# Seven products instead of eight for 81 pairs of row blocks, and a build-time planner for side work

## The chip, the cores and the metric

The kernel runs on one core of a Trainium2 chip. The metric is the device time of one execution in microseconds (us); three runs of the kernel before gave 1948.49 to 1948.88 us, median 1948.88. The engines are TensorE (PE, with its weight loads as PEld), VectorE (DVE), ScalarE (ACT), GpSimd (POOL) and SyncE (SP), which issues most loads.

## The reference

One encoder layer over 256 tokens with 4096 features, all in float32:

```python
h = rms_norm(x, g_mix)
c_q, c_kv, k_rope, gate_a, q_b, k_b, v_b, gate_b = split(h @ w_in)     # 4096 x 11840
q_a = rms_norm(c_q, g_q_latent) @ w_uq                                 # 16 heads, 128 + 64 rotary
k_nope, v_a = split(rms_norm(c_kv, g_kv_latent) @ w_ukv)
y_a = rms_norm(mla_attention(q_a, k, v_a), g_out_mla) * silu(gate_a)
y_b = rms_norm(dilated_mixture(q_b, k_b, v_b), g_out_dil) * silu(gate_b)
x = x + concat(y_a, y_b) @ w_out                                       # 4096 x 4096
gate = sigmoid(rms_norm(x, g_ple) @ w_ple_gate)                        # 4096 x 4096
out = rms_norm(x + (p @ w_ple) * gate, g_final)
```

## The kernel before

Every product of two float32 matrices is made from three matmuls in a faster 32-bit format. Both operands are split into a rounded part hi and a rest lo, and `mm` (L133 to L135) adds hi x hi, hi x lo and lo x hi in PSUM. Splitting is the side work that never ends: ScalarE copies the weights to hi (L115), VectorE subtracts to get lo (L116). A weight tile holds 1024 columns on 128 partitions.

Weights stream through a list of steps. Each step has a load into one of four raw buffers, a split into a slot of a ring (three slots, in places some spare buffers more), and a run on TensorE. The main loop at the end runs the steps in order and splits the weights of a later step after each (two steps ahead, up to five where the ring is longer). All engines take their instructions in the order in which the build emits them.

Steps of the older kind (`Chunk`) multiply both row tiles of the 256 tokens with up to 512 columns. The wide products are `Block`s of 1024 columns. In a block a *plain* step takes one row block of 128 weight rows in four products (12 matmuls of 512 columns). A *fast* pair takes two row blocks in seven products instead of eight, by the Strassen-Winograd scheme, as four steps with 3, 6, 6 and 6 matmuls, 21 for what two plain steps do in 24. For that, VectorE forms four differences of weight quarters (`sub`, L780), splits of these replace part of the plain splits, and the other operand needs sums made beforehand (`add_sums`, L818). The eight results of a block go to eight PSUM banks; a middle step (`d_mid` for the q, k and v blocks, opened by the copy in L636) empties four of them after the last fast step, and an end step (`d_done`, L651) the rest.

The order of stages: the latent columns (four chunks), the first gate chunk, the uq stage (the up projections of queries and keys, with the second gate chunk strewn in and the attention heads beside it; `done_uq` ends a query chunk with a copy in L478 and a rotary part that ends in L493; the heads' exponentials are in L417), two more gate chunks, six D blocks (q, k, v, in two halves), four gate chunks of the second kind with the dilated attention beside, three output blocks and two chunks, three gate blocks of the last product, and a tail.

Side work (attention heads, normalisations, turning tiles) is written as generators. `advance`, called after every step, resumes each of them once: what they emit, and when, is decided by the number of steps alone. Transposes go alternately to two PSUM banks (`turn_bank`). Fast pairs stand where a string says so, as four steps in a row, for example

```python
order = mix("CCCCSCSCSCSCSCSC" if n < 5 else "CCCCCSCCSCCSCCSC")     # S: a fast pair, C: two plain steps
```

Of the kernel before, what the change touches and what calls it, by code (L numbers as in the profile page):

```python
# [65 lines left out]

class Chunk:
# [4 lines left out]
    def __init__(self, src, nk, n, lhs, banks, done, needs=lambda j: (), per=2, ts=(0, 1), keep=None):  # L72
        self.src, self.nk, self.n, self.lhs, self.banks = src, nk, n, lhs, banks
        self.done, self.needs, self.per, self.ts, self.keep = done, needs, per, ts, keep
        self.ps = None
# [3 lines left out]
def encoder_layer(ctx: ExitStack, tc: tile.TileContext, x, p, positions, g_mix, w_in, g_q_latent, w_uq,  # L79
                  g_kv_latent, w_ukv, g_out_mla, g_out_dil, w_out, w_ple, g_ple, w_ple_gate, g_final,  # L80
                  c_inv, c_dist, out):
    nc = tc.nc
# [11 lines left out]
    def slot(tag, shape, dtype=F32):  # L94
        names[tag] = names.get(tag, 0) + 1
        return sp.tile([P, *shape], dtype, tag=tag, name=f"{tag}_{names[tag]}")

    def bank(tag, shape, bufs=1):
        names[tag] = names.get(tag, 0) + 1
        return pp.tile([P, *shape], F32, tag=tag, name=f"{tag}_{names[tag]}", bufs=bufs)  # L100
# [40 lines left out]
    make_identity(nc, ident)  # L141
# [25 lines left out]
    def turn_gains(i, at, n):  # L167
        tp = turn_bank([2 * S])
        nc.tensor.transpose(tp[:, :n], gains[:n, i], ident[:n, :n])
        yield  # L170
        nc.scalar.activation(gT[:, at:at + n], tp[:, :n], AF.Copy)

# [61 lines left out]
    flags, urgent, waiting, running = set(), [], [], []  # L234
    ticks = [0, -9]

    def spawn(task):
# [71 lines left out]
    def turn_c(bs):  # L309

        for b in bs:
            tp = turn_bank([2, S])
# [6 lines left out]
            split_rows(*(q[:, o:o + 2] for q in cT[key]), tp, G[key][:, o:o + 2])  # L319
            yield  # L320

    def done_a(i):
        def task(ps):
# [7 lines left out]
            for t in range(NT):  # L331
# [3 lines left out]
                else:  # L335
                    nc.scalar.activation(dst, ps[t], AF.Copy, scale=rx[:, t:t + 1])
            yield
# [26 lines left out]
    def latents():  # L364
# [8 lines left out]
        for _ in range(3):  # L373
            yield
        tp = turn_bank([2, S])
# [3 lines left out]
        split(pe[:, 0], pe[:, 1], tp[:, 0])  # L379
        flags.add("kpe")  # L380
# [5 lines left out]
    def attend(h, q_src, k_src, pe, v, y, dil):  # L386
# [4 lines left out]
        tp = turn_bank([4, P])  # L391
        for t in range(NT):
            nc.tensor.transpose(tp[:, t], q_src(t), ident)
            nc.tensor.transpose(tp[:, NT + t], k_src(t), ident)
        yield
        qk = slot(f"T{h % 2}", [2, 4 * P], F32R)
        split(qk[:, 0], qk[:, 1], tp.rearrange("p a b -> p (a b)"))
        if dil:
            flags.add(("read", h))
        yield  # L400
        s = bank("s", [NT, S])
        for t in range(NT):
# [3 lines left out]
            if pe is not None:  # L406
                both = pe[0]()[:, t * P:(t + 1) * P]
                nc.tensor.matmul(s[:, t], both, pe[1][0], start=False, stop=False)
                nc.tensor.matmul(s[:, t], both, pe[1][1], start=False, stop=True)
        yield  # L410
        i = h % 2
        e = E["t"][:, i]
        nmax, l, rl = E["s"][:, i, 0], E["s"][:, i, 1], E["s"][:, i, 2]
        if not dil:
            nc.vector.tensor_reduce(nmax, s, axis=AX.X, op=ALU.max, negate=True)
            for t in range(NT):
                nc.scalar.activation(e[:, t], s[:, t], AF.Exp, bias=nmax[:, t:t + 1], accum_out=l[:, t:t + 1])  # L417
        else:
            flat = "p a b -> p (a b)"
            nc.vector.scalar_tensor_tensor(e.rearrange(flat), E["d"][:, 0].rearrange(flat), -SLOPES[h],  # L420
                                           s.rearrange(flat), op0=ALU.mult, op1=ALU.add)
            nc.vector.tensor_reduce(nmax, e, axis=AX.X, op=ALU.max, negate=True)
# [17 lines left out]
        tp = turn_bank([NT, S])  # L440
        for k in range(NT):
            for t in range(NT):
                nc.tensor.transpose(tp[:, k, t * P:(t + 1) * P], e[:, t, k * P:(k + 1) * P], ident)
        yield
        pt = slot(f"T{2 + h % 2}", [2, NT, S], F32R)
        split(pt[:, 0], pt[:, 1], tp)
        if dil:
# [4 lines left out]
        o = bank("o", [S])  # L452
        for k in range(NT):
            mm(o, v(k), tuple(pt[:, i, k] for i in range(2)), k == 0, k == NT - 1)
        yield
# [3 lines left out]
        if h:  # L459
            nc.gpsimd.tensor_tensor(acc, acc, sq, op=ALU.add)  # L460
        flags.add(("head", dil, h))
# [10 lines left out]
    def done_uq(i):  # L472
        def task(ps):
# [3 lines left out]
            for t in range(NT):  # L477
                nc.scalar.activation(q[:, t].rearrange("p h c -> p (h c)"), ps[t], AF.Copy, scale=rqs[:, t:t + 1])  # L478
            both = kq[:, 512:].rearrange("p (t h d r) -> p t h d r", t=NT, h=2, d=2)
            rotate(both[:, :, :, 0], q[:, :, :, NOPE:], both[:, :, :, 1], 2)  # L480
            yield
            yield
            nc.scalar.activation(both[:, :, :, 1], both[:, :, :, 0], AF.Copy)
            yield
            tp = turn_bank([2, S])
# [4 lines left out]
            yield  # L490
            pe = slot("Q0", [2, S], F32R)
            nc.scalar.activation(pe, tp, AF.Copy)
            nc.vector.tensor_tensor(pe[ROPE:], tp[ROPE:], plain(pe[ROPE:]), op=ALU.subtract)  # L493
            pairs[i]["pe"] = pe
# [3 lines left out]
    def done_uk(i):  # L498
        def task(ps):
# [8 lines left out]
            for t in range(NT):  # L508
# [3 lines left out]
                split(v[:, 0, t], v[:, 1, t], kv[:, :, 1], sc)  # L512
            for hh in range(2):
                h = 2 * i + hh
                waiting.append(({("uq", i)}, attend(
# [5 lines left out]
                    y_rows(ya, h), False), 2))  # L521
# [10 lines left out]
    def y_stats(dil):  # L532
        while not all(("head", dil, h) in flags for h in range(HEADS)):
            yield
        yield
        tp = turn_bank([2 * S])
# [3 lines left out]
        yield from rsqrt_mean(ry[dil], tp[:, :NT], WIDTH)  # L540
        nc.vector.tensor_tensor(ry[dil], ry[dil], rxh, op=ALU.mult)
        flags.add(("ry", dil))

    U_TAGS = ("B7a", "B7b", "T5", "T6"), ("T7", "B7a", "B7b", "T4")

    def done_gate(dil, c):
        def task(ps):
            u = slot(U_TAGS[dil][c], [NT, 512])
            for t in range(NT):
                nc.scalar.activation(u[:, t], ps[t], AF.Tanh, scale=rxh[:, t:t + 1])  # L550
                nc.vector.scalar_tensor_tensor(u[:, t], u[:, t], 1.0, ps[t], op0=ALU.add, op1=ALU.mult)
                yield
            while ("ry", dil) not in flags or (c and ("turned", dil, c - 1) not in flags):
                yield
            yield
            for t in range(NT):
                nc.scalar.activation(u[:, t], u[:, t], AF.Copy, scale=ry[dil][:, t:t + 1])
            yield
            for b in range(2):
                w = u[:, :, S * b:S * (b + 1)]  # L560
                tp = turn_bank([2, S])
                for k in range(2):
                    for t in range(NT):
                        nc.tensor.transpose(tp[:, k, t * P:(t + 1) * P], w[:, t, k * P:(k + 1) * P], ident)
                if b:
                    flags.add(("turned", dil, c))
                yield
                for k in range(2):
                    h = 4 * c + 2 * b + k
                    g = G["ob" if dil else "oa"][:, h:h + 1]  # L570
                    y = yb_rows(h) if dil else by_token(y_rows(ya, h))
                    nc.vector.scalar_tensor_tensor(by_token(w[:, k]) if dil else y, y, g, by_token(tp[:, k]),
                                                   op0=ALU.mult, op1=ALU.mult)
            if not dil:
                flags.add(("gated", c))
                return
            while (("yT", 0, 3) if c == 0 else ("yT", 1, 1)) not in flags and c != 1:
                yield
            if c == 2:
                yt = [slot(b, [4, S], F32R) for b in ("B7a", "T6")]  # L580
            else:
                both = slot({0: "B3", 1: "B5", 3: "B6"}[c], [2, 4, S], F32R)
                yt = [both[:, 0], both[:, 1]]
            yT[4 + c] = yt
            for b in range(2):
                yield
# [829 lines left out]
```

## Time and profile before

| | |
|---|---|
| median of three runs | 1948.88 us |
| the profiled execution, first to last instruction | 1948.2 us |
| PE, PEld | 1926.8 us (99%), 1638.7 us (84%) |
| DVE, ACT, POOL | 1448.6 us (74%), 1062.6 us (55%), 67.9 us (3%) |
| DMA | 370.57 MB, 190 GB/s |
| chain that ended last | PE 90%, DVE 5%, ACT 3%, issue 1%, DMA 1% |

Matmuls are pipelined, so a matmul's recorded duration is longer than the distance to the next one's start, and a busy PE may still be waiting. Rows of the time line have the start and the duration in us, the engine, the source line, the operation, what it writes and reads with buffer numbers left out, the form, and in brackets the engine's idle time before it and what ended it. Rows of grouped instructions have a count, the total busy time in us, the mean duration in ns and the idle time before them. Waits have the total in us, how often, and the longest.

### The profile page before, as it was taken

The page shows a single profiled execution, that of the slowest core. Times are in us where ns is not written, and L with a number is a line of the kernel's source. Part 1 is how long each engine was busy: PE and PEld are TensorE (multiplying, and loading weights), DVE is VectorE, ACT ScalarE, POOL GpSimd, SP SyncE. Part 2 cuts the span into 40 slices and gives each one's busy share as a digit, 9 for nine tenths or more (in the row PEclk, how much of TensorE's full clock was granted, in tenths as well). Part 3 has the DMA queues.
Part 4 walks back from the last instruction along what each step waited for, and adds up shares of the span by engine and source line. Part 5 has one row for each costly group of instructions (what it writes and reads, how often), then busy time and mean ns, then how long its engine had stood idle before and what let it go on. Part 6 is the DMA issues. An engine that isn't in the chain of part 4 may idle for free.

```text
span 1948.2 us, 25425 instructions
## 1 busy us (share of the span) xinstructions
PE 1926.8 (99%) x9335; PEld 1638.7 (84%) x9335; DVE 1448.6 (74%) x1973; ACT 1062.6 (55%) x1459; POOL 67.9 (3%) x124
## 2 busy tenths in 40 slices
PE   9999999999999999999999999999999999999997
PEld 8998888888888888888888888888888878888887
DVE  7645566667787887878677778888876688888765
ACT  6544555555554555545456666555554455655543
POOL 1001111100000000000000010000000000000000
PEclk9999999999999999999999999999999999999999
DMA  7666545455666655656664456665566556565655
GB/s 250 187 190 195 161 140 152 135 153 180 194 202 199 223 187 195 216 191 208 204 194 143 141 153 220 220 212 184 189 194 220 185 179 221 185 224 198 223 179 180
DMA packets 150573, 370.57 MB, mean 190 GB/s; under 512 B 11925, under 2 KB 45809, under 8 KB 150193
## 3 DMA queue, kind: packets, MB, share of 16 engines
q1 hardware_dynamic: 148528, 361.80, 58.2%
q0 software_dynamic: 1920, 7.15, 1.1%
q8 instruction: 73, 1.20, 0.2%
q14 instruction: 52, 0.42, 0.1%
HBM read 364.72 MB, written 4.19 MB: 189 GB/s over the span
## 4 chain that ended last, share of the span: by engine, by line
PE 90%; DVE 5%; ACT 3%; issue 1%; DMA 1%; SPq 0%; DVEq 0%; ACTq 0%
PE m L134 20%; PE m L135 19%; PE m L133 19%; PE t L133 4%; PE t L135 4%; PE t L134 4%; PE o L135 3%; PE o L134 3%; PE o L133 3%; PE s L133 3%; PE s L135 3%; PE s L134 3%; DVE lo L116 2%; ACT hi L115 1%; ACT T L417 1%
## 5 line engine op out<-in xcount | busy, mean ns | idle before, releaser
L116 DVE TENSOR_TENSOR lo<-raw,hi 128x1024 fp32r<-128x1024 f32 (+3 forms) x507 | 570.9, 1134 | 243.7 <-ACT hi L115 241.3
L115 ACT ACTIVATE hi<-raw 128x1024 fp32r<-128x1024 f32 (+3 forms) x507 | 495.9, 987 | 303.2 <-PE m L135 120.0
L133 PE MATMUL m<-hi,Ah 128*128 128x512 f32 (+2 forms) x1203 | 458.0, 381 | 1.7 <-ACT Ah L125 0.9
L134 PE MATMUL m<-lo,Ah 128*128 128x512 f32 (+2 forms) x1203 | 452.8, 376 | 2.8 <-DVE lo L116 2.0
L135 PE MATMUL m<-hi,Al 128*128 128x512 f32 (+2 forms) x1199 | 450.1, 375 | 0.0
L134 PEld LDWEIGHTS m<-lo,Ah 128*128 128x128 f32 x1203 | 226.6, 188 | 37.7 <-DVE lo L116 4.3
L133 PEld LDWEIGHTS m<-hi,Ah 128*128 128x128 f32 x1203 | 226.5, 188 | 35.2 <-issue 1.5
L135 PEld LDWEIGHTS m<-hi,Al 128*128 128x128 f32 x1199 | 225.5, 188 | 35.8 <-DVE Al L127 0.2
L133 PE MATMUL m<-hi,B 128*128 128x512 f32 (+1 forms) x403 | 153.9, 382 | 0.0
L134 PE MATMUL m<-lo,B 128*128 128x512 f32 (+1 forms) x403 | 151.8, 377 | 1.4 <-DVE lo L116 0.6
L135 PE MATMUL m<-hi,B 128*128 128x512 f32 (+1 forms) x403 | 150.3, 373 | 0.0
L116 DVE TENSOR_TENSOR B<-raw,B 128x1024 fp32r<-128x1024 f32 (+1 forms) x81 | 87.1, 1089 | 32.9 <-ACT B L115 32.9
L115 ACT ACTIVATE B<-raw 128x1024 fp32r<-128x1024 f32 (+1 forms) x81 | 75.7, 950 | 50.0 <-PE o L135 28.0
L134 PEld LDWEIGHTS m<-lo,B 128*128 128x128 f32 x403 | 75.9, 188 | 15.3 <-DVE lo L116 5.5
L135 PEld LDWEIGHTS m<-hi,B 128*128 128x128 f32 x403 | 75.8, 188 | 10.8
L133 PEld LDWEIGHTS m<-hi,B 128*128 128x128 f32 x403 | 75.8, 188 | 9.9
L116 DVE TENSOR_TENSOR T<-t,T 128x512 fp32r<-128x512 f32 (+1 forms) x65 | 44.6, 686 | 52.0 <-ACT T L115 51.7
L793 ACT ACTIVATE hi<-raw 128x1024 fp32r<-128x1024 f32 x44 | 46.8, 1063 | 50.9 <-PE t L135 20.7
L115 ACT ACTIVATE hi<-B 128x1024 fp32r<-128x1024 f32 x44 | 46.7, 1061 | 43.1 <-PE o L135 30.9
L135 PE MATMUL m<-B,Al 128*128 128x512 f32 (+1 forms) x184 | 68.3, 371 | 0.0
L134 PE MATMUL m<-B,Ah 128*128 128x512 f32 (+1 forms) x184 | 68.3, 371 | 0.0
L133 PE MATMUL m<-B,Ah 128*128 128x512 f32 (+1 forms) x184 | 68.3, 371 | 0.0
(693 smaller groups left out, 3550.0 us busy)
## 6 DMA issues: line engine op xcount, KB each, us to landing
raw<-in_w_in_dram SPq DMA_DIRECT2D x320, 512.0 KB, 3.9
raw<-in_w_out_dram SPq DMA_DIRECT2D x128, 512.0 KB, 4.6
raw<-in_w_ple_gate_dram SPq DMA_DIRECT2D x128, 512.0 KB, 4.5
raw<-in_w_in_dram SPq DMA_DIRECT2D x63, 400.0 KB, 3.8
raw<-in_w_uq_dram SPq DMA_DIRECT2D x32, 384.0 KB, 3.4
raw<-in_w_ukv_dram SPq DMA_DIRECT2D x16, 512.0 KB, 4.6
T<-in_x_dram SPq DMA_DIRECT2D x7, 512.0 KB, 4.7
T<-in_x_dram POOLq DMA_DIRECT2D x7, 512.0 KB, 7.4
```

What stands on the lines that cost most here:

```text
L115: nc.scalar.activation(hi, src, AF.Copy)
L116: nc.vector.tensor_tensor(lo, src, plain(hi), op=ALU.subtract)
L133: nc.tensor.matmul(ps, ah, bh, start=start, stop=False)
L134: nc.tensor.matmul(ps, ah, bl, start=False, stop=False)
L135: nc.tensor.matmul(ps, al, bh, start=False, stop=stop)
L417: nc.scalar.activation(e[:, t], s[:, t], AF.Exp, bias=nmax[:, t:t + 1], accum_out=l[:, t:t + 1])
L793: nc.scalar.activation(hi, r[1], AF.Copy)
```

## The change

Four things change; the arithmetic outside the products stays as it was, and every byte loaded is the same.

1. *More fast pairs.* The first two gate chunks become one block of 1024 columns with 6 fast pairs, ahead of the uq stage, with an own set of sums; the third gate chunk takes their place inside the uq stage. The six D blocks have 6, 8, 8, 8, 8 and 4 fast pairs instead of 6, 6, 6, 6, 6 and 4, the three output blocks 4, 7 and 4 instead of 4, 6 and 4. The last three blocks keep 6 each.
2. *Spread out.* `spread` strews the four steps of each fast pair singly among the plain steps, by a running debt of VectorE time, in place of the strings.
3. *A clock at build time.* `Clock` and `Metered` stand between the kernel and the engines and keep, for each engine, an estimate of when it will be free, and for each tile when it was last written and read. Side tasks yield the time at which their inputs should be ready, and `advance` resumes a task only when TensorE's estimate has come that far. Banks and buffers that tasks share are locked (`take`, `give`, `turned`). All instructions now pass through one line, L174.
4. *Conversions by slack.* If the estimated slack of the next weights is under 4 us, they are split before side tasks are advanced, and tasks marked lazy (the sums, the last gains) wait. A ring slot is taken by who used it last, under rules when each spare buffer is open.

```diff
+    def run(self, engine, us, outs, ins, late=0.0):
+        at = self.free[engine]
+        for ap in ins:
+            at = max(at, self.after(ap, engine, True))
+        for ap in outs:
+            at = max(at, self.after(ap, engine, False))
+        self.free[engine] = at + us
...
+    def turned():
+        while True:
+            open_ = [t for t in turns if t not in locks]
+            if open_:
+                tag = min(open_, key=clock.ready)
+                locks.add(tag)
+                yield clock.ready(tag)
+                return tag
+            yield
...
-    def advance():
-        ticks[0] += 1
-        if waiting and len(running) < 5 and ticks[0] - ticks[1] >= waiting[0][2] and waiting[0][0] <= flags:
-            running.append(waiting.pop(0)[1])
-            ticks[1] = ticks[0]
+    def advance(force=False, spare=True):
+        if force:
+            ahead = [due.get(t, 0.0) for pool in (urgent, running) for t in pool]
+            now = clock.free["pe"]
+            clock.free["pe"] = max(now, min([d for d in ahead if d > now], default=now))
+        now = clock.free["pe"]
+        if waiting and len(running) < 5 and now - begun[0] >= waiting[0][2] and waiting[0][0] <= flags:
...
         for pool in (urgent, running):
             for task in list(pool):
-                if next(task, "end") == "end":
-                    pool.remove(task)
+                if due.get(task, 0.0) <= clock.free["pe"] + SOON and (spare or force or task not in lazy):
+                    resume(pool, task)
...
+    FAST_COST, PLAIN_COST, PLAIN_TIME = (1.8, 2.3, 1.15, 1.15), 1.15, 2.73
+    FAST_TIME = 0.69, 1.37, 1.37, 1.37
+    def spread(n, lead, trail, extra=()):
+        rest = 32 - 2 * n - lead - trail
+        order, debt, k = ["c"] * lead, 0.0, 0
+        rate = (n * sum(FAST_COST) + rest * PLAIN_COST) / (n * sum(FAST_TIME) + rest * PLAIN_TIME)
+        while k < 4 * n or rest:
+            if k < 4 * n and (debt <= 0 or not rest):
+                order.append("f")
+                debt += FAST_COST[k % 4] - rate * FAST_TIME[k % 4]
+                k += 1
+            else:
+                order.append("c")
+                rest -= 1
+                debt += PLAIN_COST - rate * PLAIN_TIME
...
+    FAST_GA = 6
+    hook(20, lambda: spawn(add_sums(FAST_GA, x_pair, z0_dst, ("T2", "T3"), "x_sums0", x_s0), True))
+    order = spread(FAST_GA, 10, 4)
+    blk = Block(cols(w_in, OFF_GA, 1024), lhs_x, x_s0, "x_sums0", order, lambda kt: (), Y_BANKS, ("T2", "T3"),
+                WP + [("B7a", "B7b"), ("T4", "T5")])
+    blk.key, blk.fast_needs = "ga0", ["latents", "kpe"]
...
-        order = mix("CCCCSCSCSCSCSCSC" if n < 5 else "CCCCCSCCSCCSCCSC")
+        order = spread((6, 8, 8, 8, 8, 4)[n], (10, 4, 4, 4, 4, 8)[n], 2)
+        blk.fast_needs = [("gated", 3)] if n == 0 else []
...
-        order = mix(("CCCCCCSCSCSCSCCC", "CCCSCSCSCSCSCSCC", "CCCSCCSCCSCCSCCC")[k])
+        order = spread(*((4, 8, 4), (7, 5, 4), (4, 4, 4))[k])
...
+        open_ = [tag for tag in dict.fromkeys(st.ring) if allowed.get((tag, st.ring_id), lambda i: True)(i)]
+        tag = min(open_, key=last)
...
-        while not all(f in flags for f in step.needs):
-            advance()
+        while not all(f in flags for f in step.needs) or any(b in locks for b in step.banks):
+            advance(True)
...
         step.run(*halves.pop(i))
         ran[0] = i
         if step.after:
             spawn(step.after())
-        advance()
+            advance()
+        while slack(i) < MARGIN and convert_one(lead + 1):
+            pass
+        advance(spare=slack(i) > MARGIN)
         convert(lead + 1)
```

More of the change, by code (lines that the diff above doesn't have):

```diff
@@ L490, in task @@
             yield
+            while i and not all(("scored", 0, 2 * i - 1 - n) in flags for n in range(2)):
+                yield
             pe = slot("Q0", [2, S], F32R)
@@ L551, in task @@
                 nc.vector.scalar_tensor_tensor(u[:, t], u[:, t], 1.0, ps[t], op0=ALU.add, op1=ALU.mult)
+                give(ps.tags[t])
                 yield
[L553 to L573 removed]
@@ L574, in task @@
[L574 to L586, printed above, removed]
-                split(*(q[:, 2 * b:2 * b + 2] for q in yt), u[:, :, S * b:S * (b + 1)])
```

560 lines of the change are left out of this document (435 added, 125 removed).

## The prediction

> **What bounds the kernel now.** The page's engine totals come first, then its slices.
>
> ```profile
> span 1948.2 us, 25425 instructions
> PE 1926.8 (99%) x9335; PEld 1638.7 (84%) x9335; DVE 1448.6 (74%) x1973; ACT 1062.6 (55%) x1459; POOL 67.9 (3%) x124
> ...
> PEclk9999999999999999999999999999999999999999
> DMA  7666545455666655656664456665566556565655
> ```
>
> TensorE is never long without work, and its clock is granted in full. But a busy share of 99% does not say that it streams at its pace, so the second view is its time line. Columns: start, duration, engine, line, operation, tiles, form.
>
> ```profile
> 703.17 0.39 PE L133 MATMUL m<-B,Ah 128*128 128x512 f32 x1
> 703.39 0.39 PE L134 MATMUL m<-B,Ah 128*128 128x512 f32 x1
> 703.62 0.39 PE L135 MATMUL m<-B,Al 128*128 128x512 f32 x1
> 703.85 0.39 PE L133 MATMUL m<-hi,Ah 128*128 128x512 f32 x1
> ...
> 249.09 0.28 PE L133 MATMUL o<-T,B 128*128 128x256 f32 x1
> 249.21 0.28 PE L134 MATMUL o<-T,B 128*128 128x256 f32 x1
> 249.33 0.28 PE L135 MATMUL o<-T,B 128*128 128x256 f32 x1
> 249.44 0.60 PE L443 MATMUL t<-ident,T 128*128 128x128 f32 x4
> 249.80 0.42 PE L133 MATMUL m<-hi,B 128*128 128x384 f32 x1
> 250.34 0.44 PE L134 MATMUL m<-lo,B 128*128 128x384 f32 x1
> 250.62 0.34 PE L135 MATMUL m<-hi,B 128*128 128x384 f32 x1
> 250.80 0.34 PE L133 MATMUL m<-hi,B 128*128 128x384 f32 x1
> ```
>
> Recorded durations overlap; what counts is the distance of starts. It is (703.85 - 703.17) / 3 = 0.227 us at 512 columns, 0.12 at 256, 0.18 or a little less at 384. At 249.80 the next start is 0.54 away instead of 0.17: the matmul with lo waited although the engine counts as busy. Third, the stages (length, then busy time and instructions of PE, PEld, DVE, ACT, POOL, then clock, DMA share, GB/s):
>
> ```profile
> 200.00:405.00 205.00, 203.84 (x1131) 180.05 (x1130) 124.34 (x183) 112.23 (x220) 32.10 (x67) 1.00 0.48 146
> 500.00:583.00 83.00, 83.00 (x371) 68.79 (x370) 66.93 (x76) 46.87 (x51) 0.00 (x0) 1.00 0.62 200
> 583.00:666.00 83.00, 83.00 (x368) 68.77 (x367) 68.81 (x78) 44.56 (x47) 0.00 (x0) 1.00 0.62 203
> 1580.00:1850.00 270.00, 268.27 (x1178) 220.52 (x1177) 227.53 (x276) 158.17 (x188) 1.10 (x2) 1.00 0.63 208
> 1936.00:1949.00 13.00, 0.00 (x0) 0.00 (x0) 5.69 (x21) 1.81 (x3) 0.00 (x0) 0.70 0.42 161
> ...
> L636 ACT ACTIVATE B<-m,st x10: 667/674/682, 582.6 to 998.0; 128x512 f32<-128x512 f32 x10
> L493 DVE TENSOR_TENSOR Q<-t,Q x8: 694/694/694, 224.7 to 410.0; 64x512 fp32r<-64x512 f32 x8
> ```
>
> L636 opens the middle step of each of the six D blocks (q, k, v, two halves), so five blocks take 998.0 - 582.6 = 415.4, 83.1 each. One such block before has 6 fast pairs of 21 and 10 plain pairs of 24 matmuls: 366 x 0.227 = 83.1. These blocks lose nothing. The uq stage does: L493 comes once per head pair, (410.0 - 224.7) / 7 = 26.5 apart. Its work per head pair is 48 matmuls of 384 columns (8.4), 48 of 512 (10.9), 32 of 256 for two heads (3.8) and 20 transposes (about 2.1 by the rows at 249.44 to 249.80): 25.2. About 1.2 us is lost each time, some 10 over eight. At the end 13 us pass without TensorE; that tail's code is untouched.
>
> **The change, part by part.** Counts come from the two programs' instructions in their order on each engine.
>
> *Fifteen more fast pairs.* 45 matmuls of 512 columns fewer (6,807 to 6,762, no other form changes): 45 x 0.227 = -10.2 us. All of it is on the path, since TensorE is the path. The Trainium skill (TensorE: Matmul & The Clock Gate, section Back-to-back issue gap) gives about 131 ns for a sustained 512-column matmul and 216 alone; by these the term would be 5.9 or 9.7, both estimates from that page. The rows above say 227, and they decide.
>
> *What pays for it is VectorE.* Rows of one fast pair and one plain stretch, then the groups:
>
> ```profile
> 611.35 2.36 DVE L116 TENSOR_TENSOR B<-raw,B 128x1024 fp32r<-128x1024 f32 x2 [1.50 <-ACT B L115]
> 613.62 0.69 DVE L780 TENSOR_TENSOR B<-raw 128x512 f32<-128x512 f32 x1
> 614.23 0.69 DVE L780 TENSOR_TENSOR B<-raw,raw 128x512 f32<-128x512 f32 x1
> 614.83 0.69 DVE L116 TENSOR_TENSOR lo<-raw,hi 128x512 fp32r<-128x512 f32 x1
> ...
> L116 DVE TENSOR_TENSOR lo<-raw,hi 128x1024 fp32r<-128x1024 f32 x370 | 449.0, 1224 | 199.4 <-ACT hi L115 197.8
> L818 DVE TENSOR_TENSOR B<-B 128x128 f32<-128x128 f32 x48 | 11.9, 288 | 0.8
> L651 DVE SCALAR_TENSOR_TENSOR B<-m,st,B x10: 741/744/747, 589.6 to 1005.3; 128x512 f32<-128x512 f32 x10
> ```
>
> Back to back, 1024 columns take (613.62 - 611.35) / 2 = 1.135 and 512 take 0.60; 128 I put at 0.20, the duration less the same 0.09 overlap. A fast pair is four subtractions, one half split and three whole ones: 5 x 0.60 + 3 x 1.135 = 6.4 us of VectorE beside 21 x 0.227 = 4.8 of TensorE; a plain pair is 2.3 beside 5.5. So 15 pairs add 15 x 4.1 = 62. Ten more sets of sums (28 instead of 18), each two of 512 and four of 128, add 20; the gate block's middle and end add 8 x 0.6 = 5. Together 87 us, ScalarE some 28. Hidden or not is decided per block. A D block of 8 fast pairs: 8 x 6.4 + 8 x 2.3 + 9 evacuations of about 0.66 = 75.5 of VectorE against 360 x 0.227 = 81.8 (the same sum for 6 pairs gives 67.3, and the window 583 to 666 has 68.8, so it is 1.5 short). Four blocks stand at 92 to 94%. The first D block also takes the eight sums (16) and the rest of two gates (3): 67 + 19 = 86, against 86.2 of TensorE: full. The gate block (6 pairs) is at 68 of 84, the second output block (7 pairs) at 77 of 84, the others as before. What smooths it: conversions still run up to five steps ahead, 48 steps in 81.8 us, so some 8 us, and fast and plain steps now alternate one by one, not four fast steps in a row. What is late next if VectorE falls behind is a block's middle step, and behind it the next block's first matmuls, which need its banks: two plain steps, 5.5 us, cover its 3.3. I take +2 us, nearly all in the first D block; between 0 (the sums fit into the gate stage before, VectorE 62% of TensorE) and +8 (the 16 us of sums all late, less the 8 us that the conversions run ahead).
>
> *The planner in the uq stage.* How conversions are late there:
>
> ```profile
> 234.72 1.10 ACT L478 ACTIVATE T<-m,st 128x384 f32<-128x384 f32 x2 [4.24 <-PE m L135]
> 235.72 0.47 ACT L417 ACTIVATE T<-s,st 128x256 f32<-128x256 f32 x1
> 236.62 0.60 ACT L115 ACTIVATE T<-t 128x512 fp32r<-128x512 f32 x1
> 237.10 1.07 ACT L115 ACTIVATE hi<-raw 128x1024 fp32r<-128x1024 f32 x1
> ...
> ACT T L478 <- PE m L135: 29.0, 8, 4.2
> ```
>
> ScalarE sits 4.2 us before the copy of the finished uq chunk; behind it queue two exponentials, an attention split and only then the next weights' hi, so VectorE's lo comes just in time or 0.4 late. In the changed program the exponentials stand a step before that copy, and in most steps the conversion precedes the side work; ring and lead (two steps) are as they were. ScalarE still waits for the same matmul before the same copy, so not all of the 10 us goes. I take -6, between 0 and -10.
>
> *Order around the new gate block and the first D block.* Two gate chunks become one block ahead of the uq stage; it needs the latents, and the D block's first fast step needs the last gate turned. At three steps the build runs out of ready work and places side tasks early (seven times in all, before none), so a transpose or a bank can hold TensorE up there. Nearest row: the 0.54 at 249.80 on one side; on the other, ScalarE's 4.24 wait, once. I take +1, between 0 and +4.
>
> *Moved loads.* 725 SP instructions before and after, the same bytes; 32 loads become 1024 columns wide. A pair's second raw tile is held longer, by one plain step. Landing takes 3.9 us:
>
> ```profile
> raw<-in_w_in_dram SPq DMA_DIRECT2D x320, 512.0 KB, 3.9
> ACT hi L115 <- PE o L135: 134.4, 99, 4.4
> ACT hi L115 <- DMA raw<-in_w_in_dram: 9.9, 7, 3.9
> ```
>
> With loads up to eight steps ahead I take 0; uncovered it is one landing per block at most, 3.9 x 7 = 27, but only 9.9 us of ScalarE's waiting ends on such a load today.
>
> *Sum.* 1948.2 - 10.2 + 2 - 6 + 1 = 1935.0 for the profiled span. The runs' median, 1948.88, is 0.7 above that span, so I predict 1935.7 us.
>
> **Rivals.** (a) *VectorE's waiting does not shrink, and it becomes the bound.* In the window 583 to 666 it idles 14.2 us. If a share s of that stays in every full block, the four D blocks lose 14.2s - 6.3 each, the first 14.2s, the output block 14.2s - 7: 85s - 32. All of it kept gives +53, some 1987 us; it decides at s = 0.60, where the loss is 19: with the 1 us of the forced places that takes both gains and 3.9 more. Against it: in the waits above hi ends mostly on a TensorE release, that is, on a full ring: slack, not latency. Chance 0.08. (b) *VectorE's operations stop overlapping* and each costs its full duration, 1.224, 0.69, 0.29: a D block of 8 is 8 x 7.1 + 8 x 2.45 + 6.7 = 83.1 against 81.8, the first 99 against 86, the output block 85.4 against 84.2; 5 + 13 + 1 = 19 instead of my 2, and 1952.7. The starts at 611.35 and 613.62 lie 0.09 closer than the durations, which is against it: chance 0.02. The Trainium skill (VectorE: DVE Perf Modes, section The DRAIN you can't avoid) states just that, the next operation not starting before the pipe is empty; the rows do not bear it out. (c) *The planner repairs nothing:* without the -6 the sum is 1941.7, with +4 for the forced places 1944.7. For it: ScalarE's 29.0 us stay. Chance 0.16. (d) *The gain is given back* by 10 to 17 us of stalls in the first D block and at block ends: no change, 1945 to 1953. Chance 0.07. (e) *Everything is repaired:* -10 and no new stall, 1928.7 us; chance 0.07.
>
> **How the numbers follow.** The forecast, 1930 to 1941, has 0.60. Some 0.2% (3.9 us) is what a measurement of this kernel can tell from no change. Faster: 0.60 + 0.16 + 0.07 = 0.83; same 0.07 (d) and a part of (b), 0.08; slower (a) and the rest of (b), 0.09. The range from 1926 to 1946 leaves out (a), (b) and most of (d).
>
> **What would show it.** TensorE with 9,290 matmuls; D blocks of 8 pairs 81.8 us apart, VectorE at 76 to 78 in each; the first one within 2 us of 86; the uq period down from 26.5 to about 25.7; the tail still 13. I am wrong if VectorE has no idle left in the D blocks and TensorE waits on lo there, if the uq period stays, or if TensorE stands for several us where the first D block begins.

## The result and the profile after

The changed kernel takes 1940.29 us in the median (1940.04 to 1940.43), the kernel before 1948.88 beside it (1948.49 to 1950.7). The ratio is 0.9953, with a 95% interval of 0.9939 to 0.9967: 8.6 us less, faster by more than the 0.2% that can be told here. The forecast was 1935.7, so 4.6 us of the expected gain are missing.

First the page of the changed kernel (totals and granted clock). All its instructions pass through one source line, so every row below has L174 and is told apart by its tiles.

```profile
span 1938.7 us, 25562 instructions
...
PE 1914.6 (99%) x9290; PEld 1630.6 (84%) x9290; DVE 1540.0 (79%) x2131; ACT 1093.8 (56%) x1500; POOL 81.2 (4%) x124
...
PEclk9999999999999999999999999999999999999998
```

TensorE has 45 matmuls fewer and keeps its full clock; VectorE has 91 us more (1540.0 against 1448.6). TensorE is at 99% as before, which again hides the question. The stages answer it (length, then busy time and instructions of PE, PEld, DVE, ACT, POOL, then clock, DMA share, GB/s): the uq stage, the new order around the last gate chunk, the first D block and two of 8 pairs, the output blocks, the tail.

```profile
236.00:441.00 205.00, 201.75 (x1138) 181.28 (x1136) 127.68 (x191) 116.36 (x224) 40.05 (x67) 1.00 0.49 148
441.00:497.00 56.00, 54.68 (x270) 45.68 (x271) 37.19 (x69) 29.48 (x48) 4.54 (x4) 1.00 0.54 160
497.00:578.50 81.50, 80.37 (x368) 66.11 (x367) 80.53 (x116) 49.97 (x57) 0.00 (x0) 1.00 0.62 190
578.50:660.00 81.50, 81.50 (x361) 67.50 (x360) 77.70 (x91) 47.99 (x52) 0.00 (x0) 1.00 0.66 208
660.00:741.00 81.00, 81.00 (x359) 67.05 (x358) 77.92 (x90) 48.14 (x51) 0.00 (x0) 1.00 0.67 211
1226.00:1434.00 208.00, 207.04 (x928) 170.58 (x928) 181.01 (x226) 118.27 (x145) 2.89 (x4) 1.00 0.66 208
1925.80:1938.70 12.90, 0.00 (x0) 0.00 (x0) 6.35 (x23) 1.81 (x3) 0.00 (x0) 0.59 0.48 183
```

The blocks of 8 pairs run without a gap, with VectorE at 77.7 of 81.5. To see where the rest went, I took the distance of each matmul's start to the next in both traces and subtracted the pace of its form (rounded: 0.227 us at 512 columns, 0.180 at 400, 0.174 at 384, 0.120 at 256, 0.109 for a transpose). The paces alone sum to 1910.4 before and 1900.2 after; what is left over is lost between matmuls:

| | before | after | change |
|---|---|---|---|
| work at these paces | 1910.4 | 1900.2 | -10.2 |
| lost in the uq stage | 10.1 | 7.7 | -2.4 |
| lost in the gate steps after it and the first D block | -0.2 | 2.5 | +2.7 |
| lost in the output blocks | 0.7 | 1.9 | +1.2 |
| lost in all other stretches | | | -1.3 |
| after the last matmul | 12.2 | 12.9 | +0.6 |

Such a row moves by some tenths, the third by up to 1 us, with where a stage is cut and with the third digit of a pace. Cut at 415 and 583 before and at 445 and 578.5 after, with 0.2272 at 512 columns, the third row is 0.4 and 3.4. The fourth row also moves with the execution: in a second trace of the changed kernel (`after_again`, span 1936.7) the stages up to 1226 lose the same to 0.1, but the window of the output blocks 0.7 less:

```profile
1226.00:1434.00 208.00, 207.62 (x932) 171.21 (x931) 181.09 (x227) 118.09 (x146) 2.89 (x4) 1.00 0.65 209
```

So most of its +1.2 belongs to that one execution. The changes sum to -9.4, against -9.5 of the two spans. The medians differ by 8.6 only, because the profiled execution of before was a longish one. In the later runs of both kernels the time is 1.7 to 1.8 us above that run's own span, and a median of 1948.88 belongs to a span near 1947.1, not 1948.2.

### The profile page after: what moved, and what is told of

Same layout as the page of the kernel before. It is cut to its first block, busy times and chain, and to the rows that moved or that the text cites. A ratio compares the mean times of both kernels' runs of the same rounds, so it can differ in the third digit from the quotient of the medians.

```text
span 1938.7 us, 25562 instructions
## 1 busy us (share of the span) xinstructions
PE 1914.6 (99%) x9290; PEld 1630.6 (84%) x9290; DVE 1540.0 (79%) x2131; ACT 1093.8 (56%) x1500; POOL 81.2 (4%) x124
## 4 chain that ended last, share of the span: by engine, by line
PE 89%; DVE 6%; DMA 2%; ACT 2%; issue 1%; DVEq 0%; ACTq 0%; POOLq 0%
PE m L174 51%; PE t L174 17%; PE s L174 11%; PE o L174 10%; DVE lo L174 2%; DVE B L174 1%; DVE T L174 1%; DMA raw<-in_w_ple_gate_dram 1%; ACT hi L174 1%; DMA raw<-in_w_out_dram 1%; DVE Al L174 1%; DMA raw_e<-in_w_ple_dram 0%; DVE st L174 0%; DVE Ah L174 0%; ACT B L174 0%
## 5 line engine op out<-in xcount | busy, mean ns | idle before, releaser
L174 DVE TENSOR_TENSOR lo<-raw,hi 128x1024 fp32r<-128x1024 f32 (+4 forms) x501 | 559.1, 1125 | 240.8 <-ACT hi L174 239.9
L174 ACT ACTIVATE hi<-raw 128x1024 fp32r<-128x1024 f32 (+4 forms) x501 | 488.6, 981 | 423.4 <-PE m L174 146.8
L174 PE MATMUL m<-hi,Ah 128*128 128x512 f32 (+2 forms) x711 | 265.3, 373 | 1.8 <-DVE B L174 1.0
L174 PE MATMUL m<-hi,B 128*128 128x512 f32 (+1 forms) x838 | 265.6, 376 | 0.1
L174 PE MATMUL m<-hi,Al 128*128 128x512 f32 (+2 forms) x717 | 264.0, 368 | 0.0
L174 PE MATMUL m<-lo,Ah 128*128 128x512 f32 (+2 forms) x708 | 261.3, 369 | 1.3 <-DVE lo L174 1.3
L174 DVE TENSOR_TENSOR B<-raw,B 128x1024 fp32r<-128x1024 f32 (+2 forms) x238 | 210.8, 911 | 21.0 <-ACT B L174 18.5
L174 ACT ACTIVATE B<-raw 128x1024 fp32r<-128x1024 f32 (+1 forms) x126 | 121.4, 970 | 99.8 <-PE m L174 24.9
L174 PEld LDWEIGHTS m<-hi,B 128*128 128x128 f32 x838 | 156.0, 188 | 22.6 <-DVE B L174 0.5
L174 PE MATMUL m<-lo,B 128*128 128x512 f32 (+1 forms) x419 | 157.2, 375 | 3.8 <-DVE lo L174 3.8
L174 PEld LDWEIGHTS m<-hi,Ah 128*128 128x128 f32 x711 | 134.2, 189 | 20.1 <-issue 1.7
L174 PEld LDWEIGHTS m<-hi,Al 128*128 128x128 f32 x717 | 135.1, 188 | 18.2 <-DVE Al L174 0.2
L174 PEld LDWEIGHTS m<-lo,Ah 128*128 128x128 f32 x708 | 133.5, 189 | 19.6 <-DVE lo L174 3.0
L174 PE MATMUL m<-B,Ah 128*128 128x512 f32 (+1 forms) x440 | 127.9, 375 | 0.8 <-DVE B L174 0.8
L174 PE MATMUL t<-hi,Al 128*128 128x512 f32 x250 | 97.2, 390 | 0.0
L174 PE MATMUL t<-hi,Ah 128*128 128x512 f32 x246 | 97.1, 395 | 0.0
L174 ACT ACTIVATE hi<-B 128x1024 fp32r<-128x1024 f32 x74 | 77.6, 1059 | 30.3 <-PE t L174 9.8
L174 PEld LDWEIGHTS m<-B,Ah 128*128 128x128 f32 x440 | 80.4, 188 | 16.1 <-DVE B L174 0.9
L174 PE MATMUL t<-lo,Ah 128*128 128x512 f32 x240 | 93.6, 390 | 0.0
L174 PEld LDWEIGHTS m<-lo,B 128*128 128x128 f32 x419 | 78.8, 188 | 17.6 <-DVE lo L174 6.9
L174 DVE TENSOR_TENSOR lo<-B,hi 128x1024 fp32r<-128x1024 f32 x74 | 88.4, 1219 | 5.6 <-ACT hi L174 4.9
L174 PE MATMUL m<-B,Al 128*128 128x512 f32 (+1 forms) x220 | 82.2, 374 | 0.0
```

The lines of the kernel that those rows point to most:

```text
L174: return do(out, *rest, **named)
```

## The experiments

Each run stands beside runs of the kernel before on the same chip; the times are medians. Where nothing is said, a kernel does the whole computation.

### 1. Fewer fast pairs under the new order

```diff
-        order = spread((6, 8, 8, 8, 8, 4)[n], (10, 4, 4, 4, 4, 8)[n], 2)
+        order = spread((6, 6, 6, 6, 6, 4)[n], (10, 4, 4, 4, 4, 8)[n], 2)
...
-        order = spread(*((4, 8, 4), (7, 5, 4), (4, 4, 4))[k])
+        order = spread(*((4, 8, 4), (6, 5, 4), (4, 4, 4))[k])
```

> The changed kernel with nine fast pairs fewer: 6 in each of the first five D blocks and 6 in the second output block, so 72 in all; the planner, the gate block and the spreading stay. Theory (a pair is worth its three matmuls, VectorE's extra work is hidden): 9 x 3 x 0.227 = 6.1 us slower than the changed kernel's 1940.3, 1946.4, and D blocks 83.1 apart instead of 81.8. Rival (VectorE at 92 to 94% already eats part of the gain): under 4 us slower, and TensorE's losses in the D blocks fall.

Measured: 1946.14 us, ratio 0.9985 (0.9975 to 0.9994). That is 5.9 us more than the changed kernel for 9 pairs fewer; 9 x 3 x 0.227 = 6.1. A window of this run, one D block of 6 pairs:

```profile
577.00:660.00 83.00, 83.00 (x368) 68.73 (x367) 71.84 (x80) 45.84 (x48) 0.00 (x0) 1.00 0.69 215
```

TensorE is gapless here with VectorE at 71.84 of 83.0, and gapless in the changed kernel with VectorE at 77.70 of 81.5. The pairs of the D blocks are worth their matmuls in full. (The profiled execution of this run is on the short side, 1944.55; single executions of one kernel differ here by up to 3 us, so medians are compared.) With the 72 pairs left, the planner, the spreading and the gate block together bring 2.8 us, and the 6 pairs of the gate block alone should bring 4.1: so the rest of the change costs more than it repairs.

### 2. The same VectorE work, not spread out

```diff
-                order.append("f")
-                debt += FAST_COST[k % 4] - rate * FAST_TIME[k % 4]
-                k += 1
+                for _ in range(4):
+                    order.append("f")
+                    debt += FAST_COST[k % 4] - rate * FAST_TIME[k % 4]
+                    k += 1
```

> The changed kernel with the four steps of each fast pair in a row again, at the same places by the running debt, 81 pairs. Theory (five steps of lead, some 8 us, cover a pair's deficit of 6.4 us of VectorE against 4.8 of TensorE): within 1 us of 1940.3. Rival (spreading is what makes eight pairs fit): each pair of the full blocks leaves VectorE late, 5 to 15 us slower, with TensorE waiting on lo in the D blocks.

Measured: 1947.65 us, ratio 0.9995 (0.9986 to 1.0005): no change against before, 7.4 us more than the spread order. That is the amount the rival gave, but not where it put it. A window of a D block and one of the output blocks of this run:

```profile
577.00:657.00 80.00, 80.00 (x354) 66.24 (x354) 76.59 (x90) 48.57 (x51) 0.00 (x0) 1.00 0.71 215
1232.00:1440.00 208.00, 200.13 (x894) 163.73 (x893) 174.11 (x215) 114.71 (x141) 2.88 (x4) 1.00 0.61 198
```

And its longest wait there, from TensorE's time line, with the operation of VectorE that ended it:

```profile
1407.24 0.47 PE L174 MATMUL t<-B7b,Ah 128*128 128x512 f32 x1 [2.67 <-DVE Al L174]
...
1406.22 0.87 DVE L174 SCALAR_TENSOR_TENSOR Al<-t,gT,Ah 128x256 fp32r<-128x256 f32 x2
```

The D blocks need no spreading; the conversions run far enough ahead to take four fast steps together. The output blocks do: TensorE is busy for 200.13 of 208 instead of 207.04, and by the paces they lose 9.9 us instead of 1.9. The row names VectorE's writing of Al, but this matmul reads B7b and Ah, not Al. What the two share is t: a piece of the left operand was transposed into a bank t at 1400.74, VectorE reads it out at 1406.22, and the matmul is the first of its product to write into such a bank. So the wait is, as far as the names show, for a PSUM bank that side work on VectorE has not yet emptied. TensorE's idle time in these blocks is 8.0 us: 2.7 and 1.7 of it where t is written and 0.6 where o is, all behind VectorE's reading of a transposed piece; 1.3 before a transpose whose input T is late; and only 1.7 on a lo of the weights.

### 3. Without the rule on slack

```diff
-    RAW, AHEAD, START, MARGIN = 4, 2, 20, 4.0
+    RAW, AHEAD, START, MARGIN = 4, 2, 20, -1e9
```

With this margin the tasks marked lazy are never held back either.

> The changed kernel with the slack rule off: side tasks always go ahead of the next conversion, and lazy tasks are never held. The build's clock still decides when a task is due. Theory (the slack rule repaired nothing, as the uq stage lost as much as before): within 1 us of 1940.3. Rival (the rule hides the added sums and keeps the first D block whole): 3 to 10 us slower, lost in the gate block and in the first D block.

Measured: 1951.68 us, ratio 1.0014 (1.0004 to 1.0023): 11.4 us more, and behind the kernel before. Both expectations miss: the rule repairs more than either said, and most of it in the uq stage, not in the gate block or the first D block. The operation that ends each head pair, grouped by form in this run, and behind it the window of the stage:

```profile
L174 DVE TENSOR_TENSOR Q<-t,Q x8: 695/695/695, 260.4 to 451.0; 64x512 fp32r<-64x512 f32 x8
```

```profile
236.00:452.00 216.00, 206.66 (x1149) 182.02 (x1148) 131.87 (x196) 118.32 (x228) 31.50 (x68) 1.00 0.46 142
```

Its head pairs are (451.0 - 260.4) / 7 = 27.2 us apart, and the loss in the uq stage is 16.4 instead of 7.7. So the rule that splits weights first when their slack is small does work, and is worth 11 us *inside this planner*. Against the old fixed order, whose loss was 10.1, most of that only makes good what the new placing of side work costs without the rule (16.4 - 10.1 = 6.3).

### 4. The conversion ahead of a finished chunk's evacuation

In the main loop a finished step's side task is started and resumed at once, ahead of the rule on slack.

```diff
         if step.after:
             spawn(step.after())
-            advance()
         while slack(i) < MARGIN and convert_one(lead + 1):
```

> The changed kernel without the advance that follows a finished chunk at once: the next weights are converted first if slack is short, then the chunk's evacuation. Theory (the 0.58 us stall at the end of each key and value chunk of the uq stage, seven times, comes from the evacuation standing ahead of the next conversion on ScalarE and VectorE): the seven stalls go, 3 to 5 us faster, 1935.5 to 1937.5. Rival (the evacuation, now later, gives the chunk's two banks back later): the stall moves to the next chunk's first matmul, within 1 us of 1940.3 or slower.

Measured: 1938.56 us, ratio 0.9946 (0.9931 to 0.9961). What it is about shows in the changed kernel's time lines, here ScalarE around the end of one uq chunk,

```profile
285.65 0.47 ACT L174 ACTIVATE B<-m,st 128x256 fp32r<-128x256 f32 x1 [2.76 <-DVE T L174]
287.07 0.47 ACT L174 ACTIVATE B<-m,st 128x256 fp32r<-128x256 f32 x1 [0.94 <-DVE T L174]
287.44 0.38 ACT L174 ACTIVATE B<-o 128x256 f32<-128x256 f32 x1
287.71 0.39 ACT L174 ACTIVATE acc<-o 128x256 f32<-128x256 f32 x1
287.97 0.86 ACT L174 ACTIVATE hi<-raw 128x768 fp32r<-128x768 f32 x1
```

and TensorE behind it:

```profile
289.12 0.42 PE L174 MATMUL m<-hi,B 128*128 128x384 f32 x1
289.88 0.44 PE L174 MATMUL m<-lo,B 128*128 128x384 f32 x1 [0.34 <-DVE lo L174]
290.16 0.34 PE L174 MATMUL m<-hi,B 128*128 128x384 f32 x1
```

The two copies that empty the banks (at 287.44 and 287.71) stand ahead of the next weights' hi (287.97), and the matmul with lo starts 0.76 after its forerunner instead of 0.17: 0.58 us lost, and the same in each of seven periods (at 263.9, 289.1, 315.0 and so on to 419.3). In this run these seven are gone, some 4 us. Others came for them, from its TensorE time line:

```profile
436.62 0.47 PE L174 MATMUL m<-hi,Ah 128*128 128x512 f32 x1 [2.18 <-DVE B L174]
```

a wait of 2.18 at the first gate step after the stage, and one of 2.47 at 523.7 in the first D block. The cause of the seven stalls is the order of emission. Taken away everywhere it costs elsewhere most of what it saves; that the later steps need their banks emptied at once is the likely reason, not a shown one. So theory and rival are each right for one stage, and the 1.7 us between the medians is no more than executions of one kernel differ by.

### 5. The same cause in the kernel before

If the order of emission is the cause, the old kernel must show it too, without any planner. The next conversion is put ahead of `advance` in its uq steps, and so ahead of all side work that `advance` emits, the evacuation among it:

```diff
+        if 80 <= i < 144:
+            convert(lead + 1)
         advance()
         convert(lead + 1)
```

> The kernel before, with one line: in the steps of its uq stage the next weights are converted ahead of side tasks. Theory (the same order of evacuation and conversion cost the kernel before its 10 us in this stage, and the planner is not needed to mend it): 4 to 8 us faster than 1948.9, so 1941 to 1945. Rival (without the build's clock the attention work that goes second is late and holds TensorE): within 2 us of 1948.9 or slower.

Measured: 1943.58 us, ratio 0.9971 (0.996 to 0.9983), 5.7 us less than the kernel before. The operation that ends each of its head pairs, the window of its uq stage, and from ScalarE's time line the wait at the chunk's copy (4.24 in the kernel before):

```profile
L493 DVE TENSOR_TENSOR Q<-t,Q x8: 694/696/697, 224.4 to 403.9; 64x512 fp32r<-64x512 f32 x8
```

```profile
200.00:400.00 200.00, 199.94 (x1131) 180.39 (x1130) 125.88 (x184) 114.48 (x220) 33.72 (x67) 1.00 0.51 152
```

```profile
234.01 1.10 ACT L478 ACTIVATE T<-m,st 128x384 f32<-128x384 f32 x2 [2.15 <-PE m L135]
```

The period is (403.9 - 224.4) / 7 = 25.6 instead of 26.5, and the loss by the paces 4.9 instead of 10.1. Two lines do in the old kernel twice what the planner did in the new one for that stage. Which part of the side work had stood in the way, evacuation, exponentials or attention splits, this run does not tell apart.

### 6. The conversion first in the uq steps only, and the tail

Two edits on the changed kernel. The immediate `advance` is left out in the steps of the uq stage (in the first of the two runs after step 176 as well); and in the last stage the pieces of the first token half are not all emitted behind those of the second (below).

```diff
-            if t == 0:
+            if t == 0 and c % 2:
                 yield
...
         if step.after:
             spawn(step.after())
-            advance()
+            if not (108 <= i < 170 or i == 176):
+                advance()
```

> The changed kernel with two edits: in the uq stage, but for its last chunk, and after the third gate chunk the next weights are converted ahead of the finished chunk's evacuation; and the first token half's ending yields after every second piece only, so that its last piece no longer stands behind the second half's. Theory (the evacuation ahead of the conversion costs the uq stage 0.58 us and some small waits seven times; at its end and in the first D block the early evacuation is needed): uq stage 5 to 6 us faster without the two stalls of 2.3 and 2.6 us that converting first everywhere brought, tail 0.6 shorter: 1933.5 to 1935.5. Rival (the stalls only move to a later wait, as they did in part when it was done everywhere): 1938 to 1940.

Measured: 1937.8 us, ratio 0.9938 (0.9924 to 0.9951). The uq loss falls from 7.7 to 3.4 and the tail to 12.2. But the stretch from 487 to 998 loses 5.7 instead of 0.7, most of it in waits like this one of TensorE as the first D block begins:

```profile
493.29 0.33 PE L174 MATMUL m<-ident,B7b 128*128 128x128 f32 x1 [1.87 <-ACT B7b L174]
```

So the gain of the stage arrives, and part of it is given back behind it, as the rival said. The second run has the condition without step 176, beside the changed kernel as it is, on the same chip:

```diff
-            if not (108 <= i < 170 or i == 176):
+            if not 108 <= i < 170:
```

> The changed kernel once more, on the chip of the next run. All theories: 1940.3 within 1 us, period of the uq stage 26.2.

> As the kernel with both edits, but after the third gate chunk the evacuation is again placed at once. Theory (the 2.0 and 1.9 us stalls that it had at the start of the first D block came from that one place, where the gate's work was pushed back): the uq stage keeps its 4 us, the first D block goes back to under 2 us of stalls: 1934.5 to 1936.5. Rival (they come from the uq stage's own shift, whatever follows): 1937 to 1938.5, as that kernel.

Measured: 1939.51 us (1938.53 to 1941.84) for the changed kernel, ratio 0.9954 (0.9942 to 0.9967); 1935.94 (1935.79 to 1939.18) with the edits, ratio 0.9938 (0.9925 to 0.9952). This is the lowest median here, 3.6 us under the changed kernel, though the two sets of times overlap at their ends. From the edited run's time lines, ScalarE at the same chunk end as above,

```profile
285.39 0.47 ACT L174 ACTIVATE B<-m,st 128x256 fp32r<-128x256 f32 x1 [3.02 <-DVE T L174]
286.81 0.47 ACT L174 ACTIVATE B<-m,st 128x256 fp32r<-128x256 f32 x1 [0.95 <-DVE T L174]
287.19 0.83 ACT L174 ACTIVATE hi<-raw 128x768 fp32r<-128x768 f32 x1
287.92 0.37 ACT L174 ACTIVATE B<-o 128x256 f32<-128x256 f32 x1
```

TensorE's matmuls behind it and, later, what is left at the first D block,

```profile
288.21 0.42 PE L174 MATMUL m<-hi,B 128*128 128x384 f32 x1
288.47 0.33 PE L174 MATMUL m<-lo,B 128*128 128x384 f32 x1
288.64 0.52 PE L174 MATMUL m<-hi,B 128*128 128x384 f32 x2
...
493.51 0.33 PE L174 MATMUL m<-ident,B7b 128*128 128x128 f32 x1 [1.87 <-ACT B7b L174]
```

and the operation that ends each head pair, grouped, in the changed kernel and then in this run:

```profile
L174 DVE TENSOR_TENSOR Q<-t,Q x8: 694/694/695, 259.7 to 443.0; 64x512 fp32r<-64x512 f32 x8
```

```profile
L174 DVE TENSOR_TENSOR Q<-t,Q x8: 694/694/695, 260.2 to 438.5; 64x512 fp32r<-64x512 f32 x8
```

Now hi stands ahead of the copies, the matmul with lo follows without a stall, and the period is (438.5 - 260.2) / 7 = 25.5 instead of the (443.0 - 259.7) / 7 = 26.2 of the changed kernel. The wait of 1.87 stays: it comes with the shift of the uq steps, not with step 176, and why the build leaves that transpose's input so late there is not settled. So the time lies where the first account put it, but its reason did not hold, and the times with and without step 176 (1936.09 to 1938.68, 1935.79 to 1939.18) do not tell the two runs apart.

### 7. How much room VectorE has

One difference of a fast pair (512 columns, 0.60 us) is computed twice, and then three times, in the 42 fast pairs of the D blocks; the output is unchanged.

```diff
-                sub(T[0][:, 0], r[0][:, 1], r[0][:, 0])
+                for _ in range(1 + 1 * (self.name == "x_sums")):
+                    sub(T[0][:, 0], r[0][:, 1], r[0][:, 0])
```

> The changed kernel with one of the four differences of each fast pair in the D blocks computed twice, 42 times 0.60 us more on VectorE: a block of 8 pairs stands at 80.3 of 81.8 us, the first at 90 of 86. Theory (VectorE's idle there is slack and can be filled): the four blocks keep their pace, the first loses up to 4 us: 1940 to 1944. Rival (part of the idle is latency that stays): at 0.4 of the 14 us kept each of the four blocks loses 4, 15 to 25 us slower.

> The same difference computed three times: 1.2 us more for each of the 42 pairs, 85.1 us of VectorE in a block of 8 pairs against 81.8 of TensorE, the first block 93 of 86. Theory (VectorE is the bound as soon as its sum passes TensorE's, and not earlier): four times 3.3 and the first 4 to 7: 1957 to 1961, D blocks 85 us apart. Rival (a kept share of idle): 1970 and more.

Measured: 1951.78 us, ratio 1.0013 (1.0004 to 1.0022), and 1978.2, ratio 1.0147 (1.0133 to 1.0161). One D block in a window, of the run with two,

```profile
583.40:666.40 83.00, 82.37 (x361) 67.07 (x360) 82.18 (x98) 46.92 (x52) 0.00 (x0) 1.00 0.63 202
```

and of the run with three:

```profile
588.50:677.70 89.20, 84.31 (x362) 66.95 (x361) 88.10 (x106) 46.82 (x51) 0.00 (x0) 1.00 0.60 189
```

VectorE fills up to 82.18 of 83.0 and 88.10 of 89.2: its idle time was slack and is used nearly to the end. The four blocks of 8 pairs lie between the middle steps of the first D block (578.5 in the changed kernel, 583.4 and 588.5 here) and of the fifth. ScalarE's copy that opens the fifth's, in the changed kernel, with two and with three:

```profile
906.04 1.25 ACT L174 ACTIVATE B<-m,st 128x512 f32<-128x512 f32 x2
918.44 1.25 ACT L174 ACTIVATE B<-m,st 128x512 f32<-128x512 f32 x2
945.67 1.25 ACT L174 ACTIVATE B<-m,st 128x512 f32<-128x512 f32 x2
```

The blocks are thus 81.9, 83.8 and 89.3 us apart. A repeated difference, which writes the same elements again, costs more than 0.60 us: it does not overlap with the one before. VectorE's rows of the run with two:

```profile
602.64 1.42 DVE L174 TENSOR_TENSOR B<-raw 128x512 f32<-128x512 f32 x2
603.97 0.68 DVE L174 TENSOR_TENSOR B<-raw,raw 128x512 f32<-128x512 f32 x1
```

The pair takes 1.33 us to the next start, so 0.73 for the added one. Eight of them are 5.8 us and cost 1.9, sixteen are 11.6 and cost 7.4: so 3.9 to 4.2 us of a block were free. The prediction's sums (75.5 of 81.8) left 6.3; the traced 77.7 of 81.5 leaves 3.8, and that is the number that holds. The first D block, already full, pays for its six additions: 4.4 us at that price, and its middle step comes at 583.4 instead of 578.5. Both expected times of the theory were too low (1940 to 1944, 1957 to 1961), because its sums were 2.2 us short in every block and priced the added operations at 0.60. With two the time, 11.5 us above the changed kernel, lies between theory and rival. With three the time lies where the rival put it, 1970 and more, but VectorE keeps 1.1 us of idle time in the block shown, not the rival's four tenths of 14.

## Why the prediction was right and wrong

The time lies inside the forecast range, 0.7 us from its upper end. The largest term, the products, came as worked out, and so did the D blocks; the uq term did not, and of the three signs of being wrong one nearly came: the uq period went from 26.5 to 26.2 only, not to 25.7.

*Products, -10.2: right.* 9,290 matmuls, 10.2 us less work at the traced paces, and experiment 1 gives 5.9 for 9 pairs where the same sum gives 6.1.

*VectorE, +2: right in the D blocks, right in size over all.* Blocks of 8 pairs are 81.9 apart (forecast 81.8) with VectorE at 77.7 to 77.9 in the two shown (forecast 76 to 78). (The prediction's 83.1 before is a tenth too long: 582.6 is the first copy of a middle step, 998.0 the second of another, and 582.6 to 997.4 gives 83.0.) The first D block loses 1.3 us in one place, the output blocks 1.2 more than before in this trace and about 0.5 in the second. The prediction's 86 us for the first D block counts from a start that it does not give; in the window 497 to 578.5 VectorE is at 80.53 of 81.5, as full as forecast. The sum over VectorE's operations was 2.2 us too small per block; some four tenths of the room that I counted were not there, yet what was left was enough. Rival (a), idle time that does not shrink, falls with experiment 7, where it shrinks to 1%. Rival (b) falls as well: at full durations a block of 8 would take 83.1, and it takes 81.9. The section that the prediction named for it (the Trainium skill, VectorE: DVE Perf Modes, section The DRAIN you can't avoid) says that the next operation does not start before the pipe is empty, but adds that an operation that is not held back starts earlier. The starts here, 0.60 us apart at a duration of 0.69, go with the addition, which the prediction left out.

*The planner in the uq stage, -6: the step that failed.* It brought 2.4 us, inside its bounds of 0 to 10 but under half of what was taken. I read that "in most steps the conversion precedes the side work", which is so; but the one place where it does not, the immediate resumption of a finished chunk's task, is just the place of the stall, 0.58 us once per head pair. I named the right row, ScalarE's wait of 4.24 before L478, and did not follow the changed loop at that very step. Experiments 5 and 6 show what the repair is worth where it is made: 5.2 of 10.1 in the old kernel, 4.3 of 7.7 in the new. This is most of what was missing, 3.6 us.

*Forced places, +1: about right.* The table's third row, +2.7, has the first D block's 1.3 in it, which is counted above; 1.4 is left. The waits of TensorE around there in the changed kernel:

```profile
439.86 0.47 PE L174 MATMUL m<-hi,Ah 128*128 128x512 f32 x1 [0.65 <-DVE B L174]
441.28 0.47 PE L174 MATMUL m<-hi,Ah 128*128 128x512 f32 x1 [0.49 <-DVE st L174]
466.45 0.51 PE L174 MATMUL m<-lo,Ah 128*128 128x512 f32 x1 [0.76 <-DVE lo L174]
499.85 0.70 PE L174 MATMUL t<-B,Ah 128*128 128x512 f32 x2 [1.13 <-DVE B L174]
```

The first two lie where the uq stage ends and are counted in its 7.7; the third lies behind the last gate chunk, the fourth at the first fast step of the D block. Whether the seven early placements are the cause of each was not tried; moved work at the end of the uq stage moved these waits too (experiments 4 and 6).

*The tail, unchanged: wrong by 0.6.* Its code is untouched, but the planner decides when its pieces are emitted. VectorE's last operations in the changed kernel:

```profile
1931.98 0.48 DVE L174 SCALAR_TENSOR_TENSOR T<-T,st,B 128x256 f32<-128x256 f32 x1
1932.38 0.35 DVE L174 TENSOR_SCALAR T<-T,st 128x256 f32<-128x256 f32 x1
1932.64 0.48 DVE L174 SCALAR_TENSOR_TENSOR T<-T,st,B 128x256 f32<-128x256 f32 x1
```

The last two are a piece of the first token half that now stands behind the second's; in the kernel before VectorE ended with the first of these three kinds. With the pieces paired as in experiment 6 the tail is 12.2 again.

*Loads, 0: right.* No wait of TensorE on a load appeared in the blocks. ScalarE waits on loads more than before (the conversions to hi on the loads of `w_in` 21.2 us instead of 9.9), and TensorE does not feel it.

*The last addition, +0.7.* The forecast added to the span the distance of the runs' median from that one profiled span. The later runs are 1.7 to 1.8 above their own spans; the profiled execution was simply some 1.1 above the median one. In spans, -13.2 was forecast and -9.5 found, where single executions of the changed kernel differ by 3 us (1938.53 to 1941.84).

Of the rivals, what came lies between the forecast and (c), "the planner repairs nothing", at 1941.7 to 1944.7: a repair of 2.4 instead of 6, the other terms near their forecasts.

## What to carry to other kernels

When a bottleneck engine is 99% busy, subtract the traced pace of each form from the distances of its starts: here that found 24 us before between the first matmul and the last, which the busy share hides, and showed stage by stage what a change gave back. Where engines take instructions in the order of emission, look at what stands between a finished accumulation and the next operands' conversion; moving the conversion ahead of the evacuation and the other side work was worth 5 us in one stage of a kernel of 1949, with two lines, while moving it in every step of the changed kernel gave back most of the gain. A planner's gain must be taken apart: its rule on slack was worth 11 us, its placing of side work without that rule cost about as much (1951.7 with 10.2 us of matmuls less than a kernel of 1948.9), and only the 45 matmuls taken away arrived in full.

## What had not been expected of the hardware

VectorE can be filled to 99% of a block (82.18 of 83.0 us, 88.10 of 89.2) before more work is paid at its full price; a block at 95% (77.70 of 81.5) still costs TensorE nothing. A difference of 512 columns that writes the same elements as the one before it starts 0.73 us behind it, where others of its size start 0.60 behind. And alternating single fast steps or four in a row made no difference to TensorE in the D blocks (80.00 busy of 80.00), while in the output blocks the same four in a row cost 8 us, most of it in waits for banks and inputs that side work on VectorE had not yet set free.
